# Sync engine of a ragged attention kernel: transposes ahead of the table read, loads ahead of stores, an owed store ahead of staging

## The chip, the cores and the metric

The kernel runs on one core of a Trainium2 chip. The metric is the device time of one execution in microseconds; the median of several runs is what counts. The engines are TensorE (PE, its weight loads shown as PEld), VectorE (DVE), ScalarE (ACT), GpSimd (POOL) and SyncE (SP). The whole change is in the program of SP, which computes nothing: it issues DMAs (loads, stores and DMA transposes), reads small tables into registers and branches.

## What is computed

Self-attention over 32 sequences of ragged length (64 to 511 rows of 512 columns), 8 heads of 64 columns. Each sequence is cut to its length, and the rows behind it are zero in the output:

```python
def reference(x, w_qkv, lengths, n_heads):
    output = np.zeros_like(x)
    for b in range(batch):
        seq_len = lengths[b]
        q, k, v = np.split(np.matmul(x[b, :seq_len], w_qkv), 3, axis=-1)
        # ... split in heads ...
        scores = scale * np.matmul(q, k.transpose(0, 2, 1))
        attn = softmax(scores)
        output[b, :seq_len] = np.matmul(attn, v)
```

## The kernel before

**Pairs.** The kernel sorts the sequences ("batches") by length, longest first, and works on them in 16 pairs. Each pair has a class N, the next size from a list at or above its longer member, and T = ceil(N / 128) row tiles. With this draw the classes are 512, 448, 384, 352, 352, 340, 320, 288 (pairs 0 to 7, four or three tiles), 256, 224, 224, 192, 160, 160 (pairs 8 to 13, two tiles) and 128, 96 (pairs 14 and 15, one tile). Every engine has its own loop over the classes and finds the next class in a small table on the chip. Inside a pair h = 0 and h = 1 name its two batches, and also the two sets of buffers.

**The pipeline.** Batch data pass through these stations, each a station ahead of the next: SP loads rows of x in fp32 into `x_nat[h]` (`load`, L1590 on); POOL casts them to fp16 in `x16[h]` (L1926); SP issues DMA transposes, one for each row tile, from `x16[h]` to `xT[h]` (`to_xT`, L1586); PE makes Q, K and V of the *next* batch from `xT` while it computes scores and attention of the current one; DVE normalises into `onat[h]`; the two column halves of `onat[h]` are stored, half 0 by ACT and half 1 by SP (`pay`, L1666, store at L1510). In a two-tile pair the store of the second batch's half 1 is *owed*: it is issued one batch later, by `pay_owed` (L1675) in the next pair.

**What SP waits for.** SP works strictly in program order. Before transposes it waits until PE no longer reads `xT[h]` (`s_xtf[h]`); before a load into `x_nat[1 - h]` until POOL has cast what was there (`s_xc[1 - h]`); before a store until DVE has filled the half (`s_of[h][1]`). All these waits are the line L1502 of one helper. PE in turn waits for the transposed data (`s_xt[h]`, 64 counts) before the first projection of a batch, and DVE waits for the store of a half (`s_od[h][j]`) before it normalises into that half again, one pair later (in one-tile pairs `attn_one` waits for both halves before its first reciprocal, L709).

**SP's tables.** `steps` has a row for each batch: the batch to load next, the class of the next pair, the batch itself, and a flag for `steady`. `read_step` reads one row into four registers (L1684); its load of registers from a table on the chip appears in the trace as TENSOR_LOAD. `cur` is the class of the next pair once the row has been read.

**SP's three paths.** `body` (L1795 on) is the general path of a pair. For a two-tile pair it first reads the rows of both batches (`read_step(0)`, `read_second`), and then `steady` (L1697 on) runs a path with fewer branches if the flag allows it (pairs 8 to 12). Pair 13 is the last with two tiles; it takes the general path, in which `only` asks whether the next pair has one tile, and then transposes one tile instead of two. The one-tile pairs 14 and 15 take `staged` (L1752 on): since there is little time there, the transposes go to a free part of `xT` early (`stage`, L1723), and POOL copies them into place (`place`, L1976) when PE has let go of `xT`.

Of the kernel before, what the change touches and what calls it, by code (L numbers as in the profile page):

```python
# [13 lines left out]
P = 128  # L14
# [17 lines left out]
CLASSES = sorted([STEP * k for k in range(3, 17)] + [DENSE_ROWS], reverse=True)  # L32
# [129 lines left out]
def kernel(  # L162
# [9 lines left out]
    B, MAXS, D = x.shape  # L172
# [32 lines left out]
    rank = sb("rank", [B, 1], FP32)  # L205
# [16 lines left out]
    steps = sb("steps", [1, B, 4], I32)  # L222
# [1277 lines left out]
    def wait_dec(e, s, n=1):  # L1500
        e.wait_ge(s, n)
        e.nop().then_inc(s, -n)  # L1502

    def batch_of(e, reg, tmp, off):
        e.reg_add(tmp, reg, off)
        e.reg_load(tmp, idx[0:1, bass.ds(e.snap(tmp, min_val=0, max_val=NR - 1), 1)])
        return e.snap(tmp, min_val=0, max_val=B - 1)
# [33 lines left out]
    with nc.Block() as block:  # L1541

        @block.sync
        def _(e):
# [11 lines left out]
            rank = e.alloc_register("rank")  # L1556
# [21 lines left out]
            def to_xT(h, N, tiles):  # L1578

                if tiles < NT:  # L1580
                    e.nop().then_inc(s_xt[h], 16 * (NT - tiles))
                for t in range(tiles):
                    tile_to_xT(h, t, min(P, -(-N // STEP) * STEP - t * P))

            def tile_to_xT(h, t, n):
                e.dma_start_transpose(  # L1586
                    out=xT[h][:, :, t * P : t * P + n], in_=x16[h][0:n, t, :]
                ).then_inc(s_xt[h], 16)

            def load(h, off, N, bi=None):  # L1590
                bi = batch_of(e, rank, tmp, off) if bi is None else bi
                full, more = divmod(N, P)
                rows = x[bass.ds(bi, 1), 0 : full * P + P, :] if more else x[
                    bass.ds(bi, 1), 0 : full * P, :]
                rows = rows.rearrange("o (t p) d -> p (o t) d", p=P)
                if full:
                    e.dma_start(
                        out=x_nat[h][:, 0:full, :], in_=rows[:, 0:full, :]
                    ).then_inc(s_xl[h], 16)
                if more:  # L1600
                    e.dma_start(
                        out=x_nat[h][0:more, full, :], in_=rows[0:more, full, :]
                    ).then_inc(s_xl[h], 16)
                if not full or not more:
                    e.nop().then_inc(s_xl[h], 16)
# [43 lines left out]
            for more in range(EARLY):  # L1649
# [15 lines left out]
            def index(h, k):  # L1665
                return e.snap(steps_r[h][k], min_val=0, max_val=B - 1)  # L1666

            def pay(h):
                wait_dec(e, s_of[h][1])
                store(e, index(h, 2), h, 1, 2)  # L1670

            def pay_owed(name, clear):
                top = nc.cur_bb
                lab, out_ = f"owed_b{name}", f"owed_x{name}"
                e.br_cmp(owed, 1, lab, out_, "IS_EQ")  # L1675
                nc.switch_bb(lab, parent=top)
                pay(1)
                if clear:
                    e.reg_mov(owed, 0)
                nc.switch_bb(out_, parent=top)  # L1680

            def read_step(h, at=None, into=None):
                at = rank if at is None else at
                e.reg_load(into or steps_r[h], steps[  # L1684
                    0:1, bass.ds(e.snap(at, min_val=0, max_val=B - 1), 1), :])

            def read_second():
                e.reg_add(second[3], rank, 1)
                read_step(1, second[3], [second[0], cur] + second[1:3])

            def take_second():
                for k, r in ((0, second[0]), (2, second[1])):
                    e.reg_mov(steps_r[1][k], r)

            second = [e.alloc_register(f"{r}_second") for r in ("ahead", "own", "steady", "rank")]

            def steady(N):  # L1697

                k, top = CLASSES.index(N), nc.cur_bb
                yes, no = f"even_b{N}", f"even_x{N}"  # L1700
                e.br_cmp(steps_r[0][3], CLASSES.index(P), yes, no, "IS_LT")
                nc.switch_bb(yes, parent=top)
                for h in range(2):
                    if h:
                        take_second()
                    wait_dec(e, s_xtf[h])
                    to_xT(h, N, 2)
                    if h == 0:
                        pay_owed(f"{N}e", False)
                    else:  # L1710
                        pay(0)
                    wait_dec(e, s_xc[1 - h])
                    load(1 - h, 5, N, index(h, 0))
# [38 lines left out]
            def staged(N):  # L1752

                k, top = CLASSES.index(N), nc.cur_bb
                yes, no = f"stage_b{N}", f"stage_x{N}"
                e.br_cmp(flat, 1, yes, no, "IS_EQ")
                nc.switch_bb(yes, parent=top)
                wait_dec(e, s_xc[1])
                stage(1, N)
                pay_owed(f"{N}s", True)  # L1760
                ahead(N, 1, 0, "s")
                e.reg_add(rank, rank, 1)
                read_step(1)
# [30 lines left out]

            def body(e, N):  # L1795
                T = -(-N // P)
                read_step(0)
                if T == 1:
                    staged(N)
                if T == 2:  # L1800
                    read_second()
                    steady(N)
                for h in range(2):
                    if h and T == 2:
                        take_second()
                    elif h:
                        read_step(h)
                    top = nc.cur_bb
                    lab, out_ = f"trans_b{N}_{h}", f"trans_x{N}_{h}"
                    if h == 0:  # L1810
                        e.br_cmp(rank, 0, lab, out_, "IS_NE")
                        nc.switch_bb(lab, parent=top)
                    wait_dec(e, s_xtf[h])
                    short = min(T, 2) - 1
                    first = CLASSES.index(P) if short else len(CLASSES)
                    only(
                        (cur, first, "IS_LT"), f"xt{N}_{h}",
                        lambda: to_xT(h, N, T), lambda h=h: to_xT(h, P, short),
                    )
                    if h == 0:  # L1820
                        nc.switch_bb(out_, parent=top)
                    if h == 0 and T <= 2:
                        pay_owed(N, T == 1)
                    elif T == 2:
                        pay(0)
                    wait_dec(e, s_xc[1 - h])
                    if h and T <= 2:
                        stage_next(N)
                    ahead(N, T, h)
                    if T > 2:  # L1830
                        wait_dec(e, s_of[h][1])
                        store(e, index(h, 2), h, 1, T)
                    e.reg_add(rank, rank, 1)
                if T == 2:
                    e.reg_mov(owed, 1)
                if T <= 2:
                    e.reg_mov(flat, 1)
# [274 lines left out]
```

## Time and profile before

| | |
|---|---|
| time, median of 3 runs | 334.46 us (334.26 to 335.16) |
| time of the profiled execution | 334.95 us |
| its span in the trace | 333.2 us |
| granted TensorE clock, mean | 0.99 |
| busy: PE, ACT, DVE, POOL | 317.2, 243.8, 202.7, 68.1 us |
| DMA: moved, mean rate | 72.42 MB, 217 GB/s |
| DMA transposes that SP issues | 80 |

The difference between the span and the time of the profiled execution, 334.95 - 333.2 = 1.75 us, lies outside the trace. Pairs 0 to 7 fill the trace up to about 238 us, the two-tile pairs 8 to 13 run from there to about 313 us, and the rest is the two one-tile pairs and the last stores. SP's DMAs are seen in the timeline as rows with the engine SPq: start, how long the issue kept SP, line, and operation. A row "x2" merges neighbours of one kind, from the start of the first to the end of the last. What stands in square brackets at a row's end is idle time of the engine just before it and what ended it; "PEq" or "DVEq" means that the engine's own sequencer was waiting or branching.

### The profile page before, as it was taken

The numbers are of one execution on the slowest core, as the hardware profiler recorded it, in microseconds if no ns is written. First come the engines' busy times: TensorE is split into PE (matmuls) and PEld (weight loads), VectorE is DVE, ScalarE is ACT, GpSimd is POOL, SyncE is SP. The second block draws the span as 40 slices with busy tenths as digits, with TensorE's granted clock in tenths as the row PEclk, the third lists the DMA queues.
The fourth block names the chain that finished last, engine by engine and source line by source line (L and its number), as shares of the span: only waits on it lengthen the run. The fifth ranks groups of instructions, "written<-read, shape, count | busy, mean of one in ns | idle before, by whom it ended". The sixth has DMA issues, their size and how long they took to land. (4 is left out here: it accounts for less than half of the span.)

```text
span 333.2 us, 12276 instructions
## 1 busy us (share of the span) xinstructions
PE 317.2 (95%) x4344; PEld 205.1 (62%) x4345; DVE 202.7 (61%) x582; ACT 243.8 (73%) x360; POOL 68.1 (20%) x130
## 2 busy tenths in 40 slices
PE   7999999999999999999999999999999999999970
PEld 2565545455555656656566676777777787777750
DVE  4666566546484575576376557665745566767661
ACT  4577788788979879778778886887677677666640
POOL 3554020201101201210220221022111131231331
PEclk9999999999999999999999999999999999999996
DMA  6957599986565996985985989998697879975751
GB/s 202 350 129 256 126 355 282 328 185 219 139 214 120 328 275 150 312 258 158 303 300 157 238 260 240 272 270 232 203 144 195 203 197 164 193 201 140 185 145 66
DMA packets 83289, 72.42 MB, mean 217 GB/s; under 512 B 41660, under 2 KB 64188, under 8 KB 83204
## 3 DMA queue, kind: packets, MB, share of 16 engines
q1 hardware_dynamic: 71332, 59.84, 69.8%
q10 hardware_dynamic: 11872, 11.54, 10.7%
q8 instruction: 42, 0.69, 0.9%
q14 instruction: 43, 0.35, 0.3%
HBM read 25.32 MB, written 36.70 MB: 186 GB/s over the span
## 5 line engine op out<-in xcount | busy, mean ns | idle before, releaser
L368 ACT ACTIVATE ep<-psc 128x896 f16<-128x896 f32 (+9 forms) x184 | 146.9, 847 | 41.6 <-PE psc L325 32.3
L325 PE MATMUL pa<-xT,w_r 128*128 128x160 f16 (+19 forms) x952 | 120.9, 276 | 2.4 <-PEq L62 1.3
L325 PEld LDWEIGHTS pa<-xT,w_r 128*128 128x128 f16 (+1 forms) x952 | 70.6, 97 | 29.9 <-issue 9.8
L325 PE MATMUL psc<-qkT 64*128 64x224 f16 (+17 forms) x700 | 66.7, 285 | 1.0 <-PEq L62 0.4
L441 DVE CAST qkT<-pa 128x512 f16<-128x512 f32 (+9 forms) x61 | 34.7, 568 | 48.4 <-PE pa L325 44.2
L409 ACT ACTIVATE ep<-psc 128x864 f16<-128x864 f32 (+3 forms) x56 | 49.7, 945 | 10.7 <-PE psc L325 6.4
L325 PE MATMUL pa<-w_r,xT 128*128 128x512 f16 (+4 forms) x324 | 56.5, 326 | 0.1
L325 PE MATMUL pav<-v_aug,ep 128*128 128x65 f16 x1236 | 54.5, 194 | 1.3 <-PEq L62 1.3
L325 PEld LDWEIGHTS pav<-v_aug,ep 128*128 128x128 f16 x1236 | 48.3, 98 | 9.8 <-issue 2.6
L325 PE MATMUL pav<-xT,w_r 64*128 64x352 f16 (+12 forms) x384 | 51.6, 306 | 0.4 <-PEq L62 0.4
L440 ACT CAST qkT<-pa 128x320 f16<-128x320 f32 (+8 forms) x72 | 33.2, 464 | 20.0 <-PE pa L325 12.6
L1932 POOL MEMSET v_aug<- 128x256 f16 x24 | 7.6, 315 | 184.6 <-POOLq L1502 184.6
L1926 POOL CAST x<-x_nat 128x1536 f16<-128x1536 f32 (+3 forms) x33 | 42.1, 1275 | 8.7 <-POOLq L1502 8.4
L325 PEld LDWEIGHTS psc<-qkT 64*128 64x128 f16 x700 | 26.5, 94 | 27.7 <-issue 17.3
L662 DVE SCALAR_TENSOR_TENSOR onat<-pav,masks,rcp 128x128 f32<-128x128 f32 (+1 forms) x117 | 40.5, 385 | 3.9 <-DVE rcp L639 1.5
L464 DVE TENSOR_TENSOR v_aug<-pa,masks 128x512 f16<-128x512 f32 (+1 forms) x44 | 29.4, 673 | 14.7 <-PE pa L325 14.0
L325 PEld LDWEIGHTS pav<-xT,w_r 64*128 64x128 f16 (+1 forms) x384 | 27.2, 95 | 12.9 <-issue 2.0
L325 PEld LDWEIGHTS pa<-w_r,xT 128*128 128x128 f16 (+2 forms) x324 | 22.3, 99 | 16.6 <-issue 4.1
L325 PE MATMUL pav<-w_r,xT 128*128 128x512 f16 (+3 forms) x132 | 27.7, 346 | 0.0
L325 PEld LDWEIGHTS pa<-v_aug,ep 128*128 128x128 f16 x556 | 20.4, 98 | 7.2 <-issue 2.8
L325 PE MATMUL pa<-v_aug,ep 128*128 128x65 f16 x556 | 23.0, 194 | 0.0
L639 DVE RECIPROCAL rcp<-pav 128x8 f32<-128x8 f32 (+2 forms) x64 | 12.5, 196 | 16.9 <-PE pav L325 14.1
(99 smaller groups left out, 175.9 us busy)
## 6 DMA issues: line engine op xcount, KB each, us to landing
out_dram<-zt SPq DMA_DIRECT2D x16, 768.0 KB, 5.9
x_nat<-in_x_dram SPq DMA_DIRECT2D x12, 512.0 KB
x_nat<-in_x_dram SPq DMA_DIRECT2D x5, 1024.0 KB
out_dram<-onat ACTq DMA_DIRECT2D x12, 384.0 KB, 4.8
out_dram<-onat SPq DMA_DIRECT2D x12, 384.0 KB, 4.8
x_nat<-in_x_dram SPq DMA_DIRECT2D x17, 256.0 KB, 5.8
out_dram<-onat ACTq DMA_DIRECT2D x15, 256.0 KB, 3.9
x_nat<-in_x_dram SPq DMA_DIRECT2D x4, 768.0 KB
```

Source lines behind the costliest of these rows:

```text
L325: return lambda e: e.matmul(o, lhsT, rhs, start=start, stop=stop)
L368: return e.activation(out=dst[at], in_=src[at], func=AF.Exp, scale=scale)
L409: lambda e, par=par, b=b: e.activation(out=ep[:, i, par, 0:T, 0:N], in_=psc_f[:, par, 0 : T * N].rearrange("p (t n) -> p t n", n=N), func= ...
L440: return lambda e: e.copy(out=dst, in_=src)
L441: return lambda e: e.tensor_copy(out=dst, in_=src)
L464: return lambda e: e.tensor_tensor(out=v_aug[h][:, t, lo // HD : lo // HD + n, 0:HD], in0=area[b][:, 0:w].rearrange("p (a d) -> p a d", d=HD),
L639: pr.add("dve", lambda e: e.reciprocal(out=rv, in_=den).then_inc(s_r, 1))
L662: ins = e.scalar_tensor_tensor(scalar=now[0][:, 1, t : t + 1], op0=ALU.mult, op1=ALU.mult, **ops)
L1926: e.tensor_copy(out=x16[h][:, 0:T, :], in_=x_nat[h][:, 0:T, :]).then_inc(s_xc[h], 1)
L1932: e.memset(v_aug[h][:, T - 1, NPAIR:NH, 0:HD], 0.0)
```

## The change

It has four parts, all in SP's program.

1. A pair of two or more tiles begins with the transposes of its first batch, and the table is read after them. Since the class of the next pair isn't known then, the question in `only` becomes `rank < B - 2` (is there a next pair) in place of `cur < class 128`. Pair 13 therefore transposes two tiles for the first batch of pair 14, 128 and 32 rows, where one tile of 128 rows is used.
2. In two-tile pairs one read takes both rows of the table into eight registers (`read_pair`), in place of two reads of four with an addition.
3. In `steady` the load of x precedes the store, in both batches; `steady` no longer has the first batch's transposes, which now pass the two compares of the general path.
4. In `staged` the owed store precedes the wait for POOL's cast and the staging transpose.

```diff
+            def read_pair():
+                e.reg_load(
+                    [steps_r[0][0], second[3]] + steps_r[0][2:] + [second[0], cur] + second[1:3],
+                    steps[0:1, bass.ds(e.snap(rank, min_val=0, max_val=B - 2), 2), :],
+                )
...
                 for h in range(2):
                     if h:
                         take_second()
-                    wait_dec(e, s_xtf[h])
-                    to_xT(h, N, 2)
+                        wait_dec(e, s_xtf[1])
+                        to_xT(1, N, 2)
+                    wait_dec(e, s_xc[1 - h])
+                    load(1 - h, 5, N, index(h, 0))
                     if h == 0:
                         pay_owed(f"{N}e", False)
                     else:
                         pay(0)
-                    wait_dec(e, s_xc[1 - h])
-                    load(1 - h, 5, N, index(h, 0))
...
+                pay_owed(f"{N}s", True)
                 wait_dec(e, s_xc[1])
                 stage(1, N)
-                pay_owed(f"{N}s", True)
...
-                    first = CLASSES.index(P) if short else len(CLASSES)
+                    cond = (cur, CLASSES.index(P)) if h and short else (rank, B - 2)
                     only(
-                        (cur, first, "IS_LT"), f"xt{N}_{h}",
-                        lambda: to_xT(h, N, T), lambda h=h: to_xT(h, P, short),
+                        (*cond, "IS_LT"), f"xt{N}_{h}",
+                        lambda: to_xT(h, N, T), lambda: to_xT(h, P, short),
                     )
...
+                if T > 1:
+                    transposes(0)
+                if T == 2:
+                    read_pair()
+                    steady(N)
+                else:
+                    read_step(0)
```

Three places show it in SP's instructions. In these rows L is the line in each kernel's own file, `x_0` and `x_1` are `x16[0]` and `x16[1]`, the sizes are rows x ..., and "ISA" is a register operation. The first place is the head of a two-tile pair of class 224 (pairs 9 and 10). Before:

```order
L1252 COMPARE_AND_BRANCH
L1685 ISA
L1684 TENSOR_LOAD steps
L1688 ISA
L1684 TENSOR_LOAD steps
L1701 COMPARE_AND_BRANCH
L1586 DMA_TRANSPOSE xT<-x_0 128x4x128
L1586 DMA_TRANSPOSE xT<-x_0 128x4x96
L1675 COMPARE_AND_BRANCH
L1666 ISA
L1510 DMA out_dram<-onat 128x2x256
```

And now, where the last transpose and its branches (L1568 to L1574) are the other arm of `only` and aren't run here:

```order
L1804 COMPARE_AND_BRANCH
L1565 COMPARE_AND_BRANCH
L1586 DMA_TRANSPOSE xT<-x_0 128x4x128
L1586 DMA_TRANSPOSE xT<-x_0 128x4x96
L1568 UNCONDITIONAL_BRANCH
L1586 DMA_TRANSPOSE xT<-x_0 128x4x128
L1574 UNCONDITIONAL_BRANCH
L1690 ISA
L1688 TENSOR_LOAD steps
L1703 COMPARE_AND_BRANCH
L1666 ISA
L1597 DMA x_nat<-in_x_dram 128x512
```

Two table reads ahead of the transposes have become one behind them, and the load of x (L1597) follows where the store (L1510) stood. The second place is the second batch of the same pair. Before:

```order
L1586 DMA_TRANSPOSE xT<-x_1 128x4x96
L1666 ISA
L1510 DMA out_dram<-onat 128x2x256
L1666 ISA
L1597 DMA x_nat<-in_x_dram 128x512
L1601 ISA
L1601 DMA x_nat<-in_x_dram 96x512
```

And now:

```order
L1586 DMA_TRANSPOSE xT<-x_1 128x4x96
L1666 ISA
L1597 DMA x_nat<-in_x_dram 128x512
L1601 ISA
L1601 DMA x_nat<-in_x_dram 96x512
L1666 ISA
L1510 DMA out_dram<-onat 128x2x256
```

The two parts of the load of x stand ahead of the store instead of behind it. The third place is the head of the first one-tile pair (class 128, pair 14). Before:

```order
L1685 ISA
L1684 TENSOR_LOAD steps
L1756 COMPARE_AND_BRANCH
L1723 DMA_TRANSPOSE xT<-x_1 128x4x128
L1675 COMPARE_AND_BRANCH
L1666 ISA
L1510 DMA out_dram<-onat 128x2x256
L1501 UNCONDITIONAL_BRANCH
L1565 COMPARE_AND_BRANCH
```

And now:

```order
L1684 TENSOR_LOAD steps
L1758 COMPARE_AND_BRANCH
L1675 COMPARE_AND_BRANCH
L1666 ISA
L1510 DMA out_dram<-onat 128x2x256
L1501 UNCONDITIONAL_BRANCH
L1725 DMA_TRANSPOSE xT<-x_1 128x4x128
L1565 COMPARE_AND_BRANCH
```

The store that the pair before owes has moved from behind the staging transpose to ahead of it. On the other engines no instruction is added, removed or moved.

More of the change, by code (lines that the diff above doesn't have):

```diff
@@ L1685, in read_step @@
                     0:1, bass.ds(e.snap(at, min_val=0, max_val=B - 1), 1), :])
-            def read_second():
-                e.reg_add(second[3], rank, 1)
-                read_step(1, second[3], [second[0], cur] + second[1:3])
+            def read_pair():
[3 more added lines that the diff above has]
+                )
             def take_second():
@@ L1796, in body, with transposes @@
                 T = -(-N // P)
[L1797 to L1807, printed above, removed]
+                def transposes(h):
                     top = nc.cur_bb
@@ L1821, in body @@
                         nc.switch_bb(out_, parent=top)
+                if T > 1:
[5 more added lines that the diff above has]
+                    read_step(0)
+                if T == 1:
+                    staged(N)
+                for h in range(2):
+                    if h and T == 2:
+                        take_second()
+                    elif h:
+                        read_step(h)
+                    if h or T == 1:
+                        transposes(h)
                     if h == 0 and T <= 2:
```

## The prediction

> **What bounds the kernel now.** First the page's shares of the span, then the busy times in three stretches (three and four tiles, two tiles, the end). The columns of the stretches are length, PE, PEld, DVE, ACT, POOL, clock, DMA share, GB/s.
>
> ```profile
> PE 317.2 (95%) x4344; PEld 205.1 (62%) x4345; DVE 202.7 (61%) x582; ACT 243.8 (73%) x360; POOL 68.1 (20%) x130
> ```
> ```profile
> 99.00:238.00 139.00, 137.68 (x2032) 90.78 (x2030) 86.67 (x274) 111.50 (x173) 22.37 (x36) 1.00 0.89 238
> 238.00:313.00 75.00, 74.64 (x1086) 56.57 (x1084) 47.71 (x129) 52.29 (x84) 18.16 (x36) 1.00 0.81 185
> 313.00:333.20 20.20, 9.60 (x172) 6.88 (x167) 8.94 (x19) 5.14 (x11) 5.50 (x12) 0.84 0.40 112
> ```
>
> PE is the bound: it idles 1.3 us of the 139 us of the long pairs, and 0.36 us of the 75 us with two tiles. SP's program can give back no more than that there. Only the last 20 us leave PE idle for half the time. So the question is which of these few idle stretches end at something that SP issues. Between 99 and 313 us PE's timeline has two where transposes land just before PE starts again on a new `xT` (the landings are worked out below):
>
> ```profile
> 204.64 1.02 PE L325 MATMUL pa<-w_r,xT 128*128 128x512 f16 x4
> 206.08 0.65 PE L325 MATMUL pav<-xT,w_r 128*128 128x288 f16 x4 [0.42 <-PEq L62]
> ```
> ```profile
> 296.17 0.45 PE L325 MATMUL psc<-qkT 64*128 64x160 f16 x8
> 296.93 0.30 PE L325 MATMUL pa<-xT,w_r 128*128 128x160 f16 x2 [0.31 <-PEq L62]
> ```
>
> They cost 0.42 us (pair 6) and 0.31 us (pair 12). Next SP itself: its waits in the two-tile stretch up to 291 us.
>
> ```profile
> SPq L1502 <- SPq L1502: 5.8, 5, 2.7
> ```
>
> From 291 to 313 us the same view has no row: SP waits for nothing there, so it is late, and the time of everything that it issues is its own. That stretch in SP's timeline:
>
> ```profile
> 290.53 0.53 SPq L1601 DMA_DIRECT2D x_nat<-in_x_dram  x1
> 293.15 2.54 SPq L1586 DMA_TRANSPOSE xT<-x  x2
> 296.08 0.41 SPq L1510 DMA_DIRECT2D out_dram<-onat  x1
> 296.76 0.36 SPq L1597 DMA_DIRECT2D x_nat<-in_x_dram  x1
> 297.32 0.34 SPq L1601 DMA_DIRECT2D x_nat<-in_x_dram  x1
> 297.93 3.22 SPq L1586 DMA_TRANSPOSE xT<-x  x2
> ```
>
> Between the last load of pair 11 (ends 291.06) and the first transposes of pair 12 (293.15) lie 2.09 us without a DMA: the loop's branches and the two table reads.
>
> **Part 1 and 2, two-tile pairs.** The table reads there, the register operation ahead of the second one, and for comparison a read of a single register (ACT's index):
>
> ```profile
> L1684 SPq TENSOR_LOAD <-steps x12: 293/316/565, 239.7 to 304.4; - x12
> L1688 SPq FUSED_REGOPS  x6: 133/138/140, 240.3 to 304.2; - x6
> ```
> ```profile
> L1506 ACTq TENSOR_LOAD <-idx x13: 278/288/596, 244.0 to 316.9; - x13
> ```
>
> Ahead of the transposes two reads go, 2 x 0.316 = 0.63 us, with 0.14 us and the small gaps about them some 0.9 us; two compares come in, with their gaps about 0.2 us. I take 0.7 us earlier for the transposes of pair 12. They land 2.3 us after their issue at best:
>
> ```profile
> DMA to landing us min/median/max: 2.3/2.5/2.6
> ```
>
> The second one starts at 293.15 + 2.54 - 1.23 = 294.46 and lands at 294.46 + 2.3 = 296.8, just ahead of PE's restart at 296.93. PE would have been ready at 296.17 + 0.45 = 296.62, so 0.7 us earlier removes the whole 0.31 us. In pairs 9 and 10, where SP waits for `s_xtf[0]` anyway, an earlier arrival buys nothing.
>
> The read now stands behind the transposes, on SP's way to the load and to the second batch. Four registers take 0.316 us and one 0.288 us, so eight should take about 0.35 us; bounds are one read (0.29) and two of the slowest (2 x 0.565 = 1.13). I take 0.35, by the nearest row. SP then saves about 0.25 us a pair net. What is late next is the second batch of pair 12: its transposes (297.93 on, the second at 299.19) land after 3.1 us at best, 302.3, and PE begins the matmuls on them in line:
>
> ```profile
> DMA to landing us min/median/max: 3.1/3.4/3.8
> ```
> ```profile
> 302.30 0.45 PE L325 MATMUL psc<-qkT 64*128 64x160 f16 x8
> ```
>
> A PE that is 0.31 us earlier meets that landing, which comes earlier only by SP's saving over pairs 11 and 12, 0.25 to 0.5 us. So I keep **-0.25 us** of the 0.31, bounds -0.31 and 0.
>
> The Trainium skill speaks against the merged read: its page "Runtime: NRT & Kernel Launch", section "Instruction fetch mechanics", gives a register load about 200 ns for each register, even in bulk. By it eight registers would take an estimated 1.6 us behind the transposes; the rows above (0.288 us for one register, 0.316 for four) don't agree.
>
> **Part 1, longer pairs.** Here the read takes longer, and it goes behind the transposes too:
>
> ```profile
> L1684 SPq TENSOR_LOAD <-steps x12: 313/898/969, 100.6 to 228.9; - x12
> ```
>
> The transposes start up to 0.9 us earlier. The one place where PE could use it is pair 6, 206.08 us. But these transposes land late for another reason:
>
> ```profile
> 198.28 3.86 SPq L1586 DMA_TRANSPOSE xT<-x  x3
> ```
> ```profile
> DMA to landing us min/median/max: 5.1/5.5/6.1
> ```
> ```profile
> DMA to landing us min/median/max: 7.0/7.0/7.0
> ```
>
> They need 5.1 to 6.1 us where 2.3 is possible, and the store that SP issued before them, at 196.28, needs 7.0 us and lands at 203.3 (the last row): they stand in line behind it, and an earlier issue puts them in the same place of the line. I take **0**, bounds -0.42 and 0; a loss is excluded since SP does no more than before in these pairs.
>
> By the Trainium skill, "DMA: Bandwidth & Descriptors", section "Queues, rings and completion order", each DMA engine takes a queue's descriptors in ring order; by it the term is 0, without it -0.42.
>
> **Part 3.** The load goes ahead by what the store took, 296.76 - 296.08 = 0.68 us, and the store back by the two loads, 297.93 - 296.76 = 1.17 us. No new wait: POOL has long cast when SP asks, and DVE writes the half of that store again only here, while it landed at 296.08 + 2.3 = 298.4:
>
> ```profile
> 301.47 0.21 DVE L639 RECIPROCAL rcp<-pav 128x8 f32<-128x8 f32 x1 [0.27 <-DVEq L62]
> ```
> ```profile
> DMA to landing us min/median/max: 2.3/2.3/2.4
> ```
>
> 3 us of cover against 1.2: **0**. The bytes ahead of the next transposes are the same. If that cover were gone, DVE's reciprocal would come later by the rest.
>
> **Pair 13's extra tile.** One more transpose keeps SP 1.25 us (its group's median; the pair's own first one is the row below), against 0.7 saved ahead of it, and SP's earlier savings. SP reaches the second batch 0 to 0.4 us later. Its transpose lands 3.6 us after 309.41, at 313.0, and PE uses it at 313.69, so 0.6 us cover it: **0**.
>
> ```profile
> 305.29 1.23 SPq L1586 DMA_TRANSPOSE xT<-x  x1
> ```
> ```profile
> 309.41 1.78 SPq L1586 DMA_TRANSPOSE xT<-x  x1
> ```
> ```profile
> 313.69 1.52 PE L325 MATMUL pa<-xT,w_r 128*128 128x96 f16 x32 [0.46 <-PEq L62]
> ```
>
> **Part 4, the end.** SP, DVE, POOL and PE in pair 14, and PE at the head of pair 15:
>
> ```profile
> 315.46 1.36 SPq L1723 DMA_TRANSPOSE xT<-x  x1
> 317.20 0.41 SPq L1510 DMA_DIRECT2D out_dram<-onat  x1
> ```
> ```profile
> 319.68 0.21 DVE L709 RECIPROCAL rcp<-pav 128x8 f32<-128x8 f32 x1 [1.52 <-DVEq L62]
> 320.81 0.74 DVE L510 TENSOR_SCALAR v_aug<-psc,masks 128x512 f16<-128x512 f32 x1
> ```
> ```profile
> 318.66 0.61 POOL L1976 COPY xT<-xT 128x512 f16<-128x512 f16 x1 [0.79 <-POOLq L1502]
> ```
> ```profile
> 317.91 0.42 PE L325 MATMUL pav<-v_aug,ep 128*128 128x65 f16 x8
> 320.20 1.52 PE L325 MATMUL pa<-xT,w_r 128*128 128x96 f16 x32 [0.27 <-PEq L62]
> 322.01 0.42 PE L325 MATMUL pav<-v_aug,ep 128*128 128x65 f16 x8 [0.28 <-PEq L62]
> ```
>
> The owed store, issued at 317.20 with a landing of 2.2 to 2.3 us like its neighbours above, lands at 319.4 to 319.5, and DVE's reciprocal follows at 319.68, though PE had its input ready at 318.33: that is DVE's 1.52 us idle. Ahead of the stage the store goes out at about 315.6 and lands at 317.9; DVE then starts at about 318.5, 1.2 us earlier. Of that PE gets only its own idle time: its attention matmuls at 322.01 wait for DVE's L510 (ends 321.55), while PE's work before them ends at 320.20 + 1.52 = 321.72. So **-0.28 us**, and behind it PE, ACT and DVE follow one another to the end, which keeps it.
>
> The price is the stage behind the store: later by 0.41 + 0.44 = 0.85 us, so POOL's copy moves from 318.66 to 319.5, and ends at 320.1 instead of 319.27. PE needs it at 320.20 less what PE has gained. I take +0.1, bounds 0 and +0.5 (if SP comes out of pair 13 0.4 later).
>
> **Sum.** 0 - 0.25 + 0 + 0 - 0.28 + 0.1 = -0.43 us. Against the profiled execution's own 334.95 us (span 333.2 and 1.75 outside) that is 334.5; that execution is 0.49 above the median, so from 334.46 the median becomes 334.0.
>
> **Rivals.**
> *More is won (333.4).* Pair 6's 0.42 goes too, and the stage costs nothing: -0.31 - 0.42 - 0.28 = -1.0. For it: shorter reads behind transposes (0.3 where 0.9 stood) let SP issue earlier in pairs 5 and 6. Against it: the line behind 7.0 us stores.
> *Slower (335.3): the read behind the transposes is dear.* It replaces two reads that were ahead, partly behind SP's wait. The point is where the read costs more than about 0.6 us (0.25 saved with 0.35). At the upper bound of 1.13 SP loses 0.5 us a pair; by the second batch of pair 12 that is 1.0 us, with 302.3 as the landing that has no cover, and it all reaches PE: 1.1 - 0.28 = +0.8. For it: 0.9 us reads in the long pairs, 1 us after a DMA's issue. Against it: 0.316 in these pairs. With the estimated 1.6 us from the Trainium skill's page above, the loss would be about 0.5 us a pair larger.
> *Nothing (334.5).* The transposes start earlier but land at the same time, and the late stage eats the 0.28.
>
> **How the numbers follow.** Forecast 0.50, more won 0.25, nothing 0.13, slower 0.12. A measurement of this kernel tells about 0.3%, 1.0 us, from no change. Over 1.0 us faster: half of "more" and a little of the forecast, 0.17; over 1.0 slower: most of "slower", 0.08; the rest 0.75. The bounds of the terms add up to -1.0 and +0.2, or 333.5 to 334.7; the range 333.1 to 335.1 adds 0.4 on each side, about half the spread of the three runs shown (334.26 to 335.16), and so holds most of "more" and a part of "slower".
>
> **What would show it.** Right: DVE's 1.52 us before L709 and PE's 0.28 before 322.01 gone; PE's 0.31 before 296.93 gone; the eight-register read near 0.35 us; pair 6's idle as before. Wrong: PE idle at 302.3, or in front of the projections at 313.7 or 320.2; a read of 0.6 us or more; SP waiting for `s_xc` or `s_of` where it didn't.

## The result, and the profile after

The changed kernel takes **336.62 us** (median of 22 runs, 334.05 to 341.26) against 334.58 us (22 runs, 331.7 to 337.71) of the kernel before: ratio 1.0067, 95% interval 1.0042 to 1.0093. It is slower by about 2 us, above the predicted range and on the other side of the kernel before. The intervals here and below leave out runs over 1.5% above a kernel's fastest; since the runs of one kernel lie up to 8 us apart, the medians of all runs stand beside them. The profiled execution of the changed kernel took 337.39 us, its span is 335.6.

The three stretches, with the same columns as before:

```profile
99.00:238.00 139.00, 138.22 (x2038) 91.39 (x2037) 87.27 (x278) 112.31 (x173) 22.83 (x38) 1.00 0.86 238
238.00:313.00 75.00, 73.83 (x1072) 55.83 (x1071) 46.53 (x123) 51.45 (x84) 17.68 (x34) 1.00 0.78 185
313.00:335.60 22.60, 11.42 (x176) 8.45 (x173) 9.29 (x20) 5.13 (x11) 5.36 (x12) 0.79 0.37 107
```

In the long pairs PE idles 0.78 us, where it was 1.32. In the two-tile pairs it idles 1.17 us, where it was 0.36. The end is 2.4 us longer than before.

**Pair 6.** PE's timeline there: the 0.42 us of idle time are gone.

```profile
204.50 1.02 PE L325 MATMUL pa<-w_r,xT 128*128 128x512 f16 x4
205.36 0.65 PE L325 MATMUL pav<-xT,w_r 128*128 128x288 f16 x4
```

**Pair 12.** PE, then SP:

```profile
295.69 0.45 PE L325 MATMUL psc<-qkT 64*128 64x160 f16 x8
296.44 0.71 PE L325 MATMUL pa<-xT,w_r 128*128 128x160 f16 x8 [0.30 <-PEq L62]
```
```profile
290.09 0.42 SPq L1510 DMA_DIRECT2D out_dram<-onat  x1
291.40 3.37 SPq L1586 DMA_TRANSPOSE xT<-x  x2
296.37 0.37 SPq L1597 DMA_DIRECT2D x_nat<-in_x_dram  x1
```

The idle 0.3 us ahead of the projections stays, though the transposes begin 1.75 us earlier (291.40, before 293.15): their issue took 3.37 us instead of 2.54. Behind them 1.60 us pass until the load (294.77 to 296.37); before, 0.39 us passed until the next DMA. The eight-register read is part of that:

```profile
L1688 SPq TENSOR_LOAD <-steps x6: 554/564/575, 242.5 to 307.1; - x6
```

0.56 us, where 0.35 was taken. The second batch is not late in this profile. Most of the new idle time of the two-tile pairs ends at DVE's `v_aug` (0.18 us at 290.94, 0.24 at 297.40 and 0.27 at 303.80); what made DVE late there stays open.

**The end of pair 13 and pair 14.** First PE before, then PE after:

```profile
316.54 1.53 PE L325 MATMUL pa<-xT,w_r 128*128 128x96 f16 x32
324.58 0.44 PE L325 MATMUL pav<-v_aug,ep 128*128 128x65 f16 x8 [1.02 <-PEq L62]
```
```profile
314.06 1.52 PE L325 MATMUL pa<-xT,w_r 128*128 128x96 f16 x32 [0.38 <-PEq L62]
316.63 0.34 PE L325 MATMUL psc<-qkT 64*128 64x96 f16 x8
319.37 2.72 PE L325 MATMUL pa<-xT,w_r 128*128 128x96 f16 x32 [2.39 <-PEq L62]
327.77 0.44 PE L325 MATMUL pav<-v_aug,ep 128*128 128x65 f16 x8 [1.02 <-PEq L62]
```

At 314.06 PE is 0.37 us later than before (313.69). At the next projections it is 2.83 later (319.37 for 316.54), after 2.39 us of idle time that were not there. They then take 2.72 us instead of 1.53, because the clock fell (column before the DMA share: 0.50):

```profile
319.40:321.40 2.00, 2.00 (x26) 2.00 (x27) 0.45 (x1) 0.00 (x0) 1.38 (x3) 0.50 0.32 110
```

What PE waited for is POOL's copy of the stage that SP issued at the end of pair 13. POOL, that SP row and ScalarE's store beside it, each after:

```profile
318.61 0.61 POOL L1986 COPY xT<-xT 128x512 f16<-128x512 f16 x1 [3.24 <-POOLq L1502]
```
```profile
313.05 1.20 SPq L1725 DMA_TRANSPOSE xT<-x  x1
```
```profile
313.23 0.41 ACTq L1510 DMA_DIRECT2D out_dram<-onat  x1
```

and the same two before:

```profile
312.18 1.21 SPq L1723 DMA_TRANSPOSE xT<-x  x1
```
```profile
313.10 0.38 ACTq L1510 DMA_DIRECT2D out_dram<-onat  x1
```

Before, the stage went out 0.92 us ahead of ScalarE's store and landed 2.6 us later; after, it went out 0.18 us ahead and took 5.3 us (the landings of the two lines, before first):

```profile
DMA to landing us min/median/max: 2.6/2.6/2.6
```
```profile
DMA to landing us min/median/max: 5.3/5.3/5.3
```

Fourteen of its sixteen shares had landed at 316.63, one more at 317.12, the last one at 318.35. In this time falls a packet of code (316.10 to 317.06); the queues from 316.0 to 317.1:

```profile
q1 hardware_dynamic: 65, 0.06, 15.6%
q8 instruction: 1, 0.02, 5.5%
q10 hardware_dynamic: 7, 0.01, 1.9%
```

One packet of queue 8 took 5.5% of 16 x 1.1 us, 0.97 us, on one DMA engine. The share of the stage that came last may have stood behind it; the records don't name the DMA engine of a packet.

### The profile page after: what moved, and what is told of

It is laid out like the page before. It is cut to its first block, busy times and chain, and to the rows that moved or that the text cites. A ratio compares the mean times of both kernels' runs of the same rounds, so it can differ in the third digit from the quotient of the medians.

```text
span 335.6 us, 12281 instructions
## 1 busy us (share of the span) xinstructions
PE 318.1 (95%) x4344; PEld 206.5 (62%) x4345; DVE 202.3 (60%) x582; ACT 243.6 (73%) x360; POOL 67.9 (20%) x130
## 5 line engine op out<-in xcount | busy, mean ns | idle before, releaser
L325 PE MATMUL pa<-xT,w_r 128*128 128x160 f16 (+19 forms) x952 | 122.4, 279 | 5.3 <-PEq L62 3.4
L325 PEld LDWEIGHTS pa<-xT,w_r 128*128 128x128 f16 (+1 forms) x952 | 71.5, 98 | 33.5 <-issue 13.5
```

Of the source, the lines that this page charges most:

```text
L325: return lambda e: e.matmul(o, lhsT, rhs, start=start, stop=stop)
```

## The experiments

Each was timed beside the kernel before on the same chip. What the expectations call the stage of pair 14's first batch is the stage of the rows above, issued at the end of pair 13 and needed by PE's projections at the head of pair 14.

### One part undone, one part alone

```diff
 a1: the changed kernel
-                    cond = (cur, CLASSES.index(P)) if h and short else (rank, B - 2)
+                    cond = (cur, CLASSES.index(P)) if h and short else (rank, B - 2 - 4 * short)
 a2: the changed kernel
-                pay_owed(f"{N}s", True)
                 wait_dec(e, s_xc[1])
                 stage(1, N)
+                pay_owed(f"{N}s", True)
 b1: the kernel before, a2's edit the other way round
 b2: the kernel before
-                        (cur, first, "IS_LT"), f"xt{N}_{h}",
+                        (*cond, "IS_LT"), f"xt{N}_{h}",     # cond as in the change
```

> The changed kernel, but pair 13 transposes one tile for its first batch, as before the change (from rank 26 on, instead of from rank 30). Theory 1, the extra tile: it keeps SP 1.2 us longer in pair 13, so the stage of pair 14's first batch goes out 0.9 us later than before, lands behind a slow ring, and PE waits for it. Then this kernel issues that stage at about 311.9 us instead of 313.05, PE's projections of pair 14 start near 316.5 instead of 319.4, and the time is 334.0 to 334.5 (ratio 0.998 to 1.000 against the kernel before). Theory 2, the stage of the second batch behind the owed store: still 336 to 336.6 (1.004 to 1.007). Theory 3, reads behind the transposes or loads ahead of stores in pairs 8 to 12: still 336.3 (1.005 to 1.007).

> The changed kernel with the stage of the second batch ahead of the owed store again (part 4 undone). Theory 1, the extra tile: the loss stays, 336 to 337 (1.005 to 1.008), since the stage that PE waits for was issued before this place. Theory 2, the stage behind the owed store: the loss goes, 334.3 to 334.7 (0.999 to 1.001). Theory 3, pairs 8 to 12: 336.3 (1.005 to 1.007).

> The kernel before with only part 4, the owed store ahead of the stage of the second batch. Theory 1, the extra tile: 334.2 to 334.5, the forecast's -0.28 + 0.1 (0.998 to 1.001). Theory 2, the stage behind the owed store: 335.5 to 336.6 (1.003 to 1.006). Theory 3, pairs 8 to 12: 334.2 to 334.6.

> The kernel before with only the second tile transposed for pair 13's first batch (1.23 us more on SP, all else as before). Theory 1, the extra tile: slower, 336 to 337 (1.004 to 1.008), with the stage of pair 14's first batch issued near 313.4 instead of 312.2 and PE idle before pair 14's projections. Theory 2 and theory 3: 334.6 (0.999 to 1.001).

| kernel | median us (before, same chip) | ratio, 95% interval |
|---|---|---|
| a1, change with one tile | 335.48 (334.24) | 1.0027 (0.9987 to 1.0066) |
| a2, change with the stage first | 337.30 (334.24) | 1.0065 (1.0028 to 1.0101) |
| b1, owed store first alone | 332.76 (334.24) | 0.9947 (0.9913 to 0.9982) |
| b2, extra tile alone | 337.59 (334.24) | 1.0082 (1.0046 to 1.0118) |

The extra tile alone is slower by as much as the whole change or more; the owed store alone is faster, by more than forecast. So theory 2 falls: a2 takes its cause out and keeps the loss, b1 puts it in and shows none. PE in b2, around the tile and at the head of pair 14:

```profile
307.74 1.05 PE L325 MATMUL pa<-xT,w_r 128*128 128x128 f16 x16 [0.24 <-PEq L62]
...
317.93 1.52 PE L325 MATMUL pa<-xT,w_r 128*128 128x96 f16 x32 [2.21 <-PEq L62]
```

First PE waits 0.24 us for the extra tile itself. Then SP, which the tile's issue kept 1.2 us, issues the stage at 311.76, and ScalarE its store at 311.89; the stage takes 5.2 us, and PE idles 2.21. It is the picture of the changed kernel. But theory 1 wanted 334.0 to 334.5 of a1, which is not settled by its interval, and its profile has idle time of PE elsewhere, 0.38 us at 291.39 and 0.50 at 292.61. So a second loss may stand in the two-tile pairs.

### What costs in the two-tile pairs

```diff
 b3: the kernel before, and b4, c1: the changed kernel with a1's edit and with stores ahead of loads again
-                    if h == 0:
-                        pay_owed(f"{N}e", False)
-                    else:
-                        pay(0)
                     wait_dec(e, s_xc[1 - h])
                     load(1 - h, 5, N, index(h, 0))
+                    if h == 0:
+                        pay_owed(f"{N}e", False)
+                    else:
+                        pay(0)
 (b3 as shown, b4 and c1 the other way round; b4 has the stage first too)
 b5: the kernel before, behind the transposes of pair 13's first batch
+                            e.reg_load(tmp, idx[0:1, 0:1])    # four times
```

> The kernel before with only part 3, loads of x ahead of the stores in pairs 8 to 12. Theory L, the store goes out 1.2 us later, beside ScalarE's store and right ahead of the next transposes, which land behind both and PE waits for them in pairs 10 to 12: slower, 336 to 337 (1.004 to 1.008), with new PE idle times between 276 and 304 us of 0.5 to 1.5 us in sum, the rest of the loss behind them. Theory R, the eight-register read (0.56 us, not 0.35) behind the transposes makes SP late: 334.2 to 334.6 (0.999 to 1.001).

> The changed kernel with its loads behind the stores again, the stage ahead of the owed store again, and one tile in pair 13: what is left of the change is the transposes ahead of the read, and the one eight-register read. Theory L: 333.9 to 334.5 (0.998 to 1.000). Theory R: 336 (1.003 to 1.007), with PE idle at the second batches of pairs 11 and 12, whose transposes SP issues later.

> The changed kernel with one tile in pair 13 and its loads behind the stores again: transposes first, the one read, and the owed store ahead of the stage. Theory L: as the owed store alone or better, 332.3 to 333.0 (0.993 to 0.996). Theory R: 335 to 335.5 (1.001 to 1.004), as with the loads first.

> The kernel before with four idle register reads (0.29 us each) on SP behind the transposes of pair 13's first batch, in the place where the extra tile stands, and no extra transfer. If the loss by the extra tile is SP's time (the stage of pair 14's first batch goes out beside ScalarE's store instead of 0.9 us ahead of it): 336.5 to 337.5 (1.005 to 1.009), with PE idle for over 2 us before pair 14's projections in most executions. If it is the extra transfer itself that holds up the rings: 334.6 (0.999 to 1.001).

| kernel | median us (before, same chip) | ratio, 95% interval |
|---|---|---|
| b3, loads first alone | 335.60 (334.16) | 1.0024 (0.9984 to 1.0064) |
| b4, transposes first and one read | 338.03 (334.16), 6 runs | 1.0130 (1.0087 to 1.0172) |
| c1, b4 and owed store first | 335.30 (334.16) | 1.0014 (0.9984 to 1.0045) |
| b5, idle reads | 335.04 (334.16) | 0.9995 (0.9959 to 1.0030) |

b3 alone decides nothing: its interval holds no change and theory L's 1.004, and its profile has idle times of the kind that theory L looked for (0.51 us at 291.42, 1.42 at 298.05). Theory L falls by the other two: b4, which leaves out the part that it blames, is the slowest kernel so far, and c1 came to 1.0014 where theory L wanted 0.993 to 0.996. b5 told nothing of a delay. Its reads, whose result is not used, don't appear in the trace; SP's store follows the tile as closely as before:

```profile
307.53 1.23 SPq L1586 DMA_TRANSPOSE xT<-x  x1
309.14 0.41 SPq L1510 DMA_DIRECT2D out_dram<-onat  x1
```

So b5 is a second run of the kernel before. It shows the size of the scatter: 0.9 us between two medians of one program.

How the early transposes may lose is seen in c1, SP and PE in pair 12:

```profile
292.15 3.13 SPq L1586 DMA_TRANSPOSE xT<-x  x2
296.98 0.43 SPq L1510 DMA_DIRECT2D out_dram<-onat  x1
297.68 1.63 SPq L1597 DMA_DIRECT2D x_nat<-in_x_dram  x1
299.50 0.34 SPq L1601 DMA_DIRECT2D x_nat<-in_x_dram  x1
300.12 2.51 SPq L1586 DMA_TRANSPOSE xT<-x  x2
```
```profile
303.92 1.27 PE L325 MATMUL pa<-xT,w_r 128*128 128x160 f16 x16 [1.49 <-PEq L62]
```

Two issues are held: the transposes for 3.13 us (2.5 is usual) and the load for 1.63 (0.36 is usual). Between them stands the read, now in the way of everything behind it. The second batch's transposes go out at 300.12, and PE waits 1.49 us. While the load is held, a packet of code moves; the queues from 297.5 to 299.0, one packet of 0.056 x 16 x 1.5 = 1.34 us:

```profile
q1 hardware_dynamic: 256, 0.25, 47.0%
q8 instruction: 1, 0.02, 5.6%
```

In the kernel before such a packet moved from 291.2 to 292.7, again one of queue 8 (291 to 293):

```profile
q1 hardware_dynamic: 202, 0.36, 47.6%
q10 hardware_dynamic: 250, 0.24, 46.8%
q8 instruction: 1, 0.02, 4.8%
q14 instruction: 1, 0.01, 1.2%
```

At that time SP was at its branches and table reads (291.1 to 293.0); the two reads took 0.33 and 0.29 us beside the packet, no more than elsewhere. So the reads may have cost nothing there, and the change put transposes into their place. That is theory C of the next runs.

### Long pairs, two-tile pairs, the read, a real delay

```diff
 d1: the kernel before; d2, d3: the changed kernel with part 3, part 4 and the extra tile undone
 d1   if T > 2: transposes(0)   then read_step(0), read_second() and, for T == 2, transposes(0)
 d2   if T == 2: transposes(0), read_pair()      long pairs read first
 d3   if T == 2: read_pair(), transposes(0)      long pairs read first
 d4: the kernel before, behind the transposes of pair 13's first batch, 18 times
+                            e.nop().then_inc(s_srt, 1 - 2 * (k % 2))
```

> The kernel before with the transposes ahead of the table read in the pairs of three and four tiles only; pairs of two tiles read first, as before. Theory C, SP's issue is held while a 16 KB packet of code is on the rings, and before the change SP's table reads in the two-tile pairs stood in that time: no loss here, 333.5 to 334.7 (0.997 to 1.001). Theory G, the loss comes with the long pairs, whose earlier transposes only push other transfers back: 336 to 338 (1.004 to 1.012).

> The other half: transposes ahead of the one eight-register read in the two-tile pairs only, long pairs as before, one tile in pair 13. Theory C: the loss of both together, 336 to 338 (1.005 to 1.013), with transposes of pairs 11 and 12 whose issue takes 1.5 to 2.9 us instead of 1.25 and SP 0.5 to 2 us later at the second batch. Theory G: 334.2 to 334.7 (0.999 to 1.001).

> The same with the eight-register read back ahead of the transposes: against the kernel before only one read of 0.56 us stands where two of 0.32 and 0.14 us of arithmetic stood. Theory C: 333.8 to 334.6 (0.998 to 1.001). If the eight-register read is dear wherever it stands (0.56 us and up to 0.42 us behind it): 335.5 to 336.5 (1.003 to 1.007).

> The kernel before with 18 semaphore instructions (about 0.07 us each, 1.2 us together) on SP behind the transposes of pair 13's first batch, where the extra tile stands, and no extra transfer. If the loss by the extra tile (1.008) is SP's time: 336.5 to 337.5 (1.005 to 1.009), with the stage of pair 14's first batch issued within 0.4 us of ScalarE's store and PE idle for 2 us before pair 14's projections. If it is the extra transfer, which PE waits for (307.61 us) and which holds the rings: 334.0 to 334.9 (0.999 to 1.002).

| kernel | median us (before, same chip) | ratio, 95% interval |
|---|---|---|
| d1, transposes first in long pairs | 335.45 (334.92) | 0.9965 (0.9927 to 1.0004) |
| d2, transposes first in two-tile pairs | 336.36 (334.92) | 1.0026 (0.9982 to 1.0070) |
| d3, one read, ahead | 334.45 (334.92) | 0.9991 (0.9963 to 1.0020) |
| d4, delay | 336.41 (334.92) | 1.0020 (0.9982 to 1.0058) |

d3 clears the eight-register read in the old place: at 0.56 us, but ahead of the transposes, it costs nothing that can be told (0.9963 to 1.0020). d1 and d2 don't decide by themselves: theory C's 1.005 for d2 and no loss at all both lie in its interval, and theory G's 1.004 for d1 does not. d4 goes the way of the extra tile, with half its price, though its interval holds no change as well. In its profile the delay did more than 1.2 us:

```profile
305.76 1.23 SPq L1586 DMA_TRANSPOSE xT<-x  x1
308.43 0.42 SPq L1510 DMA_DIRECT2D out_dram<-onat  x1
309.22 1.27 SPq L1597 DMA_DIRECT2D x_nat<-in_x_dram  x1
```
```profile
314.72 1.52 PE L325 MATMUL pa<-xT,w_r 128*128 128x96 f16 x32 [1.51 <-PEq L62]
...
318.97 1.22 PE L325 MATMUL pa<-xT,w_r 128*128 128x96 f16 x25 [1.33 <-PEq L62]
```

The delayed load met a packet of code (308.76 to 310.21) and was held 0.9 us.

### The packets of code moved

```diff
 e1: the kernel before; e2: the changed kernel
-FIRST = {4: 20, 3: 20, 2: 20, 1: 20}
+FIRST = {4: 20, 3: 20, 2: 84, 1: 20}
 e3: d3's edit of the kernel before, and the owed store ahead of the stage
```

> The kernel before with TensorE's code of the two-tile classes laid 64 instructions further on against the 256-instruction blocks in which it is fetched; every instruction of every engine stays, only the place in the pair changes at which a 16 KB packet of code is fetched (by some 2 us, at 29 instructions per us). Theory C, SP's issue is held by these packets: SP's issues of over 1.35 us move with the packets, and each still overlaps one; the time may go either way by up to 3 us. The other theory, SP's issue is held by the transfers queued ahead of it: the long issues stay at the same places of the program, and the time stays within 0.3%.

> The changed kernel with the same move of TensorE's code. Theory C: the transposes ahead of the read meet the packets at another place, so the loss of pairs 10 to 12 changes, and the distance to the kernel with the same layout but without the change is another than 2.0 us (0 to 1 or over 3 us). The other theory: 336.6, and the distance stays 2 us.

> The kernel before with the two parts that showed no loss: the owed store ahead of the stage (0.9947 alone) and the one eight-register read in the old place, ahead of the transposes (0.999 alone). If the parts add up: 332.5 to 333.2 (0.993 to 0.997), faster than both kernels. If the gain of the owed store was an accident of one position of the code packets in the tail: 334 to 335 (0.999 to 1.002).

| kernel | median us (before, same chip) | ratio, 95% interval |
|---|---|---|
| e1, code moved | 341.71 (334.76), 6 runs | 1.0203 (1.0148 to 1.0259) |
| e2, code moved in the changed kernel | 343.41 (334.76), 6 runs | 1.0245 (1.0183 to 1.0307) |
| e3, owed store first and one read | 333.29 (334.76) | 0.9972 (0.9938 to 1.0006) |

The move cost far more than meant, mostly since TensorE itself ran out of code. This is read from an idle time with the releaser "issue" (the engine waited for nothing that the profile shows), in which two packets of queue 8 move, from 246.91 to 248.81 and from 249.46 to 250.44 (e1):

```profile
251.84 1.04 PE L325 MATMUL psc<-qkT 64*128 64x256 f16 x8 [4.90 <-issue]
```

So the times of e1 and e2 say nothing of SP. Their distance, 1.7 us, can't be told from the 2.0 us between the kernels with the old layout; the expectation that it would change is not borne out. The traces do answer the question on SP. In the kernel before, long issues stood in pair 10's first batch (1.93 us) and pair 11's second (2.28), and none in pair 10's second (1.21 and 1.24) or pair 12's first (1.26 and 1.23). In e1 the first two take 1.22 and 1.23, but pair 10's second batch has one of 2.00 and pair 12's first one of 1.47. These long issues moved, and each again overlaps a packet; five others stand at the same place in both kernels, with a packet beside them in both. Counted over the traces of all 19 kernels, 238 to 325 us:

| SP's issues | beside no packet of queue 8 | beside one |
|---|---|---|
| transposes | 257, 6 over 1.35 us | 236, 144 over 1.35 us |
| loads and stores | 547, 2 over 0.6 us | 75, 51 over 0.6 us |

The long issues go with the packets. That the packet itself holds SP, and not a third thing that slows both, no run could isolate. Reads of four registers hardly follow the packets (median 0.32 us beside one, 41 of them; 0.31 beside none, 116), the few reads of eight do (1.06 us, 9 of them; 0.57 us, 57).

e3's interval holds both of its expectations, the sum of the two parts and an accident.

The Trainium skill, "Runtime: NRT & Kernel Launch", section "Instruction fetch mechanics", says that code comes in blocks of 16 KiB over a queue of the engine's own and that the cost of a block is mostly hidden. Packets of 16384 bytes in queue 8 agree with the first. For the second, TensorE's longest idle time with the releaser "issue" from 99 us on is 0.71 us in the old layout (d3) and 4.9 us in e1, and SP's issues are long beside the packets.

### Both causes taken out of the changed kernel

```diff
 f1: the changed kernel
-                if T > 1:
-                    transposes(0)
                 if T == 2:
                     read_pair()
+                if T > 1:
+                    transposes(0)
+                if T == 2:
                     steady(N)
 f2: f1 with a1's edit
```

> The changed kernel with the eight-register read back ahead of the transposes in the two-tile pairs; all else of the change stays (the extra tile, loads ahead of stores, owed store ahead of the stage, transposes first in the long pairs). If the transposes ahead of the read cost what they cost alone (+1.3 to +1.4 us): 335.0 to 335.8 (1.001 to 1.004), PE's idle of pairs 10 to 12 smaller, the 2 us in front of pair 14 still there in most executions. If all of the loss is the extra tile's: 336.6 (1.005 to 1.008).

> The same and pair 13 with one tile: both causes taken out of the changed kernel. What is left is loads ahead of stores, the owed store ahead of the stage, one read instead of two, and transposes first in the long pairs. If the two causes are the whole loss: 332.8 to 334.3 (0.994 to 1.000), as the owed store alone with what the loads first cost. If something else is in it: 335 or more (over 1.002).

| kernel | median us (before, same chip) | ratio, 95% interval |
|---|---|---|
| f1, change with the read ahead | 335.49 (334.65) | 1.0024 (0.9985 to 1.0062) |
| f2, and one tile | 335.24 (334.65) | 1.0022 (0.9979 to 1.0065) |

f1 came into its first forecast (335.0 to 335.8), though its interval holds the other's 1.005 as well. The wait in front of pair 14's projections is still there:

```profile
319.88 1.31 PE L325 MATMUL pa<-xT,w_r 128*128 128x96 f16 x27 [2.16 <-PEq L62]
```

f2 did not come down to 334.3, though its interval doesn't exclude that. In its profile, the shortest but one of all (span 330.7), PE has no such wait:

```profile
316.01 1.53 PE L325 MATMUL pa<-xT,w_r 128*128 128x96 f16 x32
```

With intervals of 0.4% each, one kernel can't settle terms of 1.5 us; all together do better. A least squares fit over the fifteen kernels without d4, e1 and e2 (with the change, and b5 as a repeat of before; means of all runs, each against before on its chip, weighted by their scatter, two standard errors) gives: transposes ahead of the read in two-tile pairs **+1.7 us** (0.6), the extra tile **+1.6** (0.7), the owed store first **-1.1** (0.5), loads first +0.3 (0.8). Over the runs that the intervals use they are +1.3, +1.7, -0.9 and +0.3. The sum is +2.5, the changed kernel's own mean +2.2 (1.0). In a fit with two more terms, transposes first in the long pairs get +0.7 (0.9) and the one read 0.0 (0.7). b2, b4 and f2 lie 1.1 to 2.1 us above the fit, so the parts don't simply add up, and the errors given are too small by about a third (the weighted squares of the misfit sum to 19.6 where 11 are expected). Every edit also moves SP's own code behind it, and no run holds that still.

## Why the prediction was wrong

**Pair 13's extra tile: 0 was taken, about +1.6 us is measured (alone +2.7 by b2's ratio, +3.3 by the medians). This is the step whose failure the traces show.** The prediction looked at the 0.6 us of cover of the transposes right behind the tile, and PE did find these in time (0.38 us idle at 314.06, 0.46 before). It didn't follow SP's queue one DMA further. The stage behind them had 0.92 us of lead on ScalarE's store, and lost it. In the traces of all 19 kernels the wait goes with this lead:

| ScalarE's store follows the stage by | kernels | the stage lands after | PE idle in front of pair 14's projections |
|---|---|---|---|
| 0.13 to 0.36 us | with the tile: the change, a2, b2, e2, f1; without: b4, e1 | 4.9 to 5.3 us | 1.9 to 2.4 us |
| 0.72 us | b3 | 3.9 us | 0.46 us |
| 0.92 to 1.25 us | before, a1, b1, b5, c1, d1, d3, f2 | 2.5 to 2.6 us | none |
| 1.34 and 1.49 us, a packet of code beside the stage's issue | d2, e3 | 4.8 and 3.7 us | 0.32 us, none |
| it goes out 1.38 us ahead | d4 (delay) | 3.8 us | 1.3 us |

So the tile's own transfer isn't needed for the wait: b4 and e1 have none, and show the same lead, landing and wait. The tile takes the lead away, since its issue keeps SP 1.2 us. d4 goes the same way, but its time alone proves nothing. Why a stage so close to the store lands so late stays open.

The wait also goes with a lower clock in a part of the executions. In the changed kernel's profile the 32 matmuls behind it take 1.2 us longer. The granted clock of a whole execution is 0.988 or less in 22 of 58 executions of the four kernels with the tile and the old code layout, and in 9 of 139 of the kernel before.

**Parts 1 and 2 in two-tile pairs: -0.25 was taken, about +1.7 is measured by the fit.** This step failed too, and it failed by its sign. The prediction counted the reads as time that the transposes would gain. In the changed kernel's profile the transposes' issue was held (3.37 us for 2.54 in pair 12): for a start 1.75 us earlier the second one landed only 0.5 us earlier (296.31, before 296.79), and PE's wait stays. The reads, moved out of time in which SP could perhaps issue little, stand in front of the second batch. This account is argued, not shown, since single profiles disagree. PE waits 1.4 to 1.7 us for one batch in a2 (pair 11's second), b4 and c1 (pair 12's second), which have the early transposes, but also in b3, d1 and e3 (pair 12's first), which don't; and d2, which has them, has no such wait. From 262 us to the end of the two-tile pairs' matmuls PE idles 1.9 us on average in the six profiles with early transposes, and 1.6 in the eleven without (old code layout). The read's own price was mis-sized, 0.56 for 0.35, but d3 shows no cost of it in the old place. The rival "the read behind the transposes is dear" (335.3) names the right place and the point of decision, 0.6 us; with 0.56 us, 1.06 beside a packet, and the time around it the read stands there.

**Part 1 in the long pairs: 0, bounds -0.42 and 0.** Pair 6's idle time is gone in the changed kernel, but in a2 0.52 us and in d1 0.40 stand at the same place. No gain is shown; d1's interval ends at 1.0004.

**Part 3: 0.** Right within what can be told: +0.3 (0.8).

**Part 4: -0.18 was taken, about -1.1 is measured; the sign is right and the size isn't.** The row of DVE's L510 didn't show the wait by itself (it ended at 321.55, ahead of PE's 321.72). But what was to be seen came: in b1 DVE's 1.52 us in front of L709 are 0.29, and PE's 0.28 us are gone:

```profile
318.08 0.21 DVE L709 RECIPROCAL rcp<-pav 128x8 f32<-128x8 f32 x1 [0.29 <-DVEq L62]
```
```profile
319.78 1.52 PE L325 MATMUL pa<-xT,w_r 128*128 128x96 f16 x32 [0.24 <-PEq L62]
321.14 0.42 PE L325 MATMUL pav<-v_aug,ep 128*128 128x65 f16 x8
```

From the projections at the head of pair 15 to the last attention matmuls PE needs 3.94 us (319.78 to 323.72), before 4.38. The other 1.8 us by which b1's profile is shorter come from the last store: one share of it landed 2.2 us late before and 0.1 late in b1. Whether part 4 makes that likelier is not settled: such a share is over 1.7 us late in three of the eight traces with part 4 and in six of the eleven without.

**The range.** All bounds came from PE's idle time in one execution, so a loss could only come from a cover that was looked at. The spread of the runs was taken from three of them, 0.9 us; over 22 runs it is 6 us.

The best kernel tried is b1, the kernel before with the owed store first: 332.76 us, 0.9947 (0.9913 to 0.9982), faster than both. It is the fastest of seventeen, so part of that may be luck; e3, which adds the one read to it, came to 0.9972 (0.9938 to 1.0006).

## What to carry to other kernels

When work is added to a queue in program order, follow every DMA behind it up to the last one that an engine waits for; the first has cover, and a later one may have none. A register read that costs nothing may be standing in time when nothing else could be issued, so look at what the DMA queues move there before something is put in its place. Where runs scatter by 2%, judge a part by several kernels that hold it, not by one profile.

## What the hardware showed unexpectedly

- SP's DMA issues are long almost only beside 16 KB packets of queue 8: 195 of 311 beside one, 8 of 804 beside none. These packets belong to TensorE's code by all that is seen: e1 moved nothing else, and TensorE idled for 4.9 us while two of them moved.
- TensorE's clock went to 0.50 behind 2.39 us of idle time in the changed kernel and behind 2.06 us in e1; the 32 matmuls took 2.72 us in both. Behind 2.21 us in b2, 2.16 in f1 and 2.10 in b4 they ran at full speed (1.52 us in b2). So the length of this one wait doesn't decide it.
- A DMA transpose landed 2.5 to 2.6 us after its issue when ScalarE's store followed 0.92 to 1.25 us later, and 4.9 to 5.3 us after it when the store followed within 0.36 us.
- A read of eight registers took 0.56 us, one of four 0.32, one of one 0.29.
